# Strassen's weight sums moved to accumulating DMAs, and one product added onto another's PSUM bank

## The chip, the core and the metric

The kernel runs on one core of one Trainium2 chip. The metric is device time in microseconds for one execution, as the median of several runs. TensorE is called PE, VectorE DVE, ScalarE ACT, GpSimd POOL and SyncE SP, as in the profile.

## The reference

One layer of a streaming encoder for 512 tokens and a model dimension of 2048, all in float32. Cut to what matters:

```python
hn   = rmsnorm(x, norm_g)                                   # (512, 2048)
proj = hn @ w_in                                            # 3 branches x (q, k, v, gate) x 4 heads x 128 columns,
                                                            # 4 forget logits, 3 x 2048 merge gate logits
ya = forgetting_attention(qa, ka, va, f_logit)              # branch A
yb = chunked_relpos_attention(qb, kb, vb, rel_bias)         # branch B
yc = stick_breaking_attention(qc, kc, vc)                   # branch C
ys = stack([ya, yb, yc]) * silu(gate path)
merged = sum over branches of sigmoid(merge gates) * (ys @ w_up)
out = x + merged @ w_out
```

Almost all arithmetic is in the projections: `hn @ w_in` (2048 x 12292), `ys @ w_up` and `merged @ w_out`.

## The kernel before

Tokens lie along the free dimension (512 columns), rows of a weight matrix along the partitions. A column tile is 128 output columns; its weights are two loads of 128 x (8 x 128) float32, 512 KB each, one for each half of the 2048 rows. Each factor is split into a high part (float32r, a rounded copy made on ACT, L92) and a low part (the difference, on DVE, L93), and a product is three matmuls, high x high, low x high and high x low (`mm3`, L100 to L103).

**Pairs.** Two column tiles are computed together by Strassen's scheme in Winograd's form (`pair_task`): seven products of half the rows by half the tokens (256 columns) in place of eight. With A11, A12 the first tile's two halves of the rows, and A21, A22 the second's, the products are numbered Q1 to Q7. Their weights are A11 (Q1), A12 (Q2), A22 (Q4) and four sums and differences (Q5, Q7, Q6, Q3). On the other side stand halves of x and differences of them, split once (`combos` for x, `merged_combos` for the merged branches). `combos` makes the differences on POOL, `merged_combos` on DVE. There are 54 pairs: 46 over the columns of `w_in` and 8 over `w_out`. One of them, the first of the output projection, is `late`, with another order of the products, since its operands with x differences are ready last.

**Units.** The work is a list of units; a unit is one stretch of PE with one stationary operand: a product of a pair (24 matmuls of 256 columns), half of a column tile as it stands (the first head's four tiles, 24 matmuls of 512 columns), or half of an up projection (18 matmuls of 512 columns). The loop at the end of `hybrid_kernel` goes over the units: it first emits the splits (`prep_to`) of up to two units ahead, then the loads (`load_to`) of up to six ahead, then the unit's matmuls, its eviction (`after`) and the stages of attention that hang on it (`side`). A scheduler orders the instructions on each engine by their dependences and its own costs; PE keeps the written order only for the first 17 units.

**Buffers.** Raw weights have six buffers (`raw`), split weights three for the high and three for the low part (`wh`, `wl`), projections four PSUM banks (`acc`), and temporaries of 128 x 512 share 21 slots (`t2`). So a split waits until PE has finished the unit three before it.

**A pair before.** All four loads are issued on SP for the first unit. On DVE, w5 = A21 + A22 (L315), w7 = w1 - w7 (L324), w6 = w5 - w1 (L325) and w3 = w3 - w6 (L327), each 128 x 1024; the late pair makes the same sums by L315, L317, L318 and L327. The order of the products is Q1, Q2, Q6, Q7, Q4, Q5, Q3. Evictions are one copy on ACT and seven additions or subtractions of 128 x 256 on DVE.

**The start.** The rows of x come in by 16 loads, are split raw, and the first head's four column tiles run on them as they stand, while the norm is found; then `combos` multiplies x by its norm (DVE, L255), makes the differences (POOL, L257 to L260), and the parts are split again (x1h, x1l, t23h, t23l, x2h, x2l). The first pair needs these.

Of the kernel before, what the change touches and what calls it, by code (L numbers as in the profile page):

```python
# [38 lines left out]
def hybrid_kernel(  # L39
# [60 lines left out]
    def mm3(ps, lh, ll, rh, rl, start, stop):  # L100
        nc.tensor.matmul(ps, lh, rh, start=start, stop=False)  # L101
        nc.tensor.matmul(ps, lh, rl, start=False, stop=False)  # L102
        nc.tensor.matmul(ps, ll, rh, start=False, stop=stop)  # L103

    # ------------------------------------------------------------------ constants
# [18 lines left out]
    class Unit:  # L124
        """A stretch of the tensor engine's work with one stationary operand of up to 8 k tiles."""

        def __init__(self, shape, prep, mms, srcs=(), after=None):
            self.shape, self.prep, self.mms, self.srcs, self.after = shape, prep, mms, srcs, after
            self.hi = self.lo = None
# [4 lines left out]
    def load(u):  # L134
        u.raw = []
        for s, keep in u.srcs:
            t = raw_tile(u.shape)
            nc.sync.dma_start(t, s)
            u.raw.append(t)
            if keep is not None:  # L140
                keep.append(t)
# [8 lines left out]
    def prep_raw(u):  # L150
        split_to(u.hi, u.lo, u.raw[0])
# [21 lines left out]
    # -1 where key k >= j: suffix sums inside a block  # L173
# [4 lines left out]
    # A, rows are queries: NEG where the key (free) is after the query  # L178
# [4 lines left out]
    # C, rows are keys: valid where the query (free) is after the key  # L183
# [7 lines left out]
    # column h has ones on the rows h, 32 + h, 64 + h, 96 + h  # L191
# [6 lines left out]
    # the query gains carry the softmax scale  # L198
# [33 lines left out]
    def rsqrt(y, ps, n):  # L232
        """y = (ps / n + EPS) ** -0.5: a guess by exp and ln, and one Newton step."""
# [17 lines left out]
    def combos(k):  # L251
        """The rows of x at their norm, and what Strassen's form needs of them beside the parts."""
# [5 lines left out]
        nc.gpsimd.tensor_sub(a[:, RH], a[:, RH], a[:, LH])  # L258
        nc.gpsimd.tensor_sub(t[:, LH], b[:, RH], a[:, RH])
# [24 lines left out]
    def col_task(srcs, xs, evac):  # L284
        """A column tile as it stands; two units, one for each half of the rows."""
        ps = Lazy(acc)

        def mms(i):
            def go(u):
                for j in range(UK):  # L290
# [4 lines left out]
                     srcs=[(srcs[i], None)],  # L295
                     after=(lambda: evac(ps())) if i == 1 else None) for i in range(2)]

    def pair_task(src1, src2, ops, done, late=False, before_last=None):
        """Two column tiles by seven products in place of eight (Strassen, in Winograd's form).

        late: the products with T2, T3 and T4 come last."""
        kept = []
        st = {}
        w = {}
        order = (1, 2, 5, 3, 6, 7, 4) if late else (1, 2, 6, 7, 4, 5, 3)

        def prep_of(i):
            p = order[i]

            def go(u):  # L310
                if i == 0:
                    w[1], a21, w[4], w[2] = kept
                    split_to(u.hi, u.lo, w[1])
                    w[5] = raw_tile()
                    nc.vector.tensor_add(w[5], a21, w[4])  # L315
                    if late:
                        nc.vector.tensor_sub(a21, w[1], a21)  # L317
                        nc.vector.tensor_sub(w[1], w[5], w[1])  # L318
                    w[7], w[6], w[3] = a21, w[1], w[2]
                    return  # L320
                split_to(u.hi, u.lo, w[p])
                if i == 1:
                    if not late:
                        nc.vector.tensor_sub(w[7], w[1], w[7])  # L324
                        nc.vector.tensor_sub(w[6], w[5], w[1])  # L325
                if i == (1 if late else 4):
                    nc.vector.tensor_sub(w[3], w[3], w[6])  # L327
            return go

        def mms_of(i):  # L330
            def go(u):
                st["ps"] = ps = acc()[:, LH]
                for j in range(UK):
                    mm3(ps, u.hi[:, j, :], u.lo[:, j, :], *ops[order[i]](j), j == 0, j == UK - 1)
            return go

        def after_of(i):
            p = order[i]

            def go():  # L340
                ps = st["ps"]
# [8 lines left out]
                elif p == 6:  # L350
                    add(u[:, LH], u[:, LH], ps)
                    if late:
                        add(c1[:, RH], c1[:, RH], u[:, LH])
                elif p == 7:
                    add(u[:, RH], u[:, LH], ps)
                    if late:
                        add(c2[:, RH], c2[:, RH], u[:, RH])
# [4 lines left out]
                elif p == 5:  # L362
# [548 lines left out]
```

## Time and profile before

| | |
|---|---|
| median of 3 runs | 1400.05 us (1399.22 to 1400.08) |
| profiled execution | span 1397.6 us from the first to the last instruction; its own whole time is not on the page |
| busy: PE, DVE, ACT, POOL | 1366.3, 1191.8, 729.7, 53.7 us |
| mean granted PE clock | 0.995 |
| moved by DMA | 176.39 MB, 126 GB/s in the mean, 38.4% of the DMA engines' time on SP's and ACT's load queue |

The span is from the first to the last instruction; busy is the time with an instruction under way. Matmuls overlap, so the pace of PE is read from the distance of their starts. A wait is shown as who waited, and for whom (`<-`); a releaser is inferred.

### The profile page before, as it was taken

The numbers are of one execution on the slowest core, as the hardware profiler recorded it, in microseconds if no ns is written. First come the engines' busy times: TensorE is split into PE (matmuls) and PEld (weight loads), VectorE is DVE, ScalarE is ACT, GpSimd is POOL, SyncE is SP. The second block draws the span as 40 slices with busy tenths as digits, with TensorE's granted clock in tenths as the row PEclk, the third lists the DMA queues.
The fourth block names the chain that finished last, engine by engine and source line by source line (L and its number), as shares of the span: only waits on it lengthen the run. The fifth ranks groups of instructions, "written<-read, shape, count | busy, mean of one in ns | idle before, by whom it ended". The sixth has DMA issues, their size and how long they took to land.

```text
span 1397.6 us, 25474 instructions
## 1 busy us (share of the span) xinstructions
PE 1366.3 (98%) x10452; PEld 1316.7 (94%) x10452; DVE 1191.8 (85%) x1671; ACT 729.7 (52%) x1042; POOL 53.7 (4%) x60
## 2 busy tenths in 40 slices
PE   6969999999999999999999999999999999999999
PEld 3759999999999999999999999999999988899999
DVE  8999898887978889888888888888888888898886
ACT  6345564544545555555556555545555755453332
POOL 4730000000000000000000000000000000000000
PEclk9989999999999999999999999999999999999999
DMA  7113334323344244342433333333233766535542
GB/s 272 46 46 106 122 102 126 121 91 114 106 129 126 95 114 128 113 129 95 117 122 115 121 94 119 113 114 121 91 115 103 273 197 203 169 109 176 164 151 76
DMA packets 63093, 176.39 MB, mean 126 GB/s; under 512 B 7400, under 2 KB 9320, under 8 KB 62976
## 3 DMA queue, kind: packets, MB, share of 16 engines
q1 hardware_dynamic: 59520, 170.49, 38.4%
q10 hardware_dynamic: 3456, 4.26, 0.8%
q8 instruction: 82, 1.34, 0.4%
q14 instruction: 35, 0.29, 0.1%
HBM read 155.04 MB, written 19.69 MB: 125 GB/s over the span
## 4 chain that ended last, share of the span: by engine, by line
PE 92%; DVE 5%; issue 1%; ACT 0%; POOL 0%; DMA 0%; SPq 0%; DVEq 0%; ACTq 0%; POOLq 0%
PE acc L101 27%; PE acc L103 27%; PE acc L102 27%; PE att L103 3%; PE att L101 3%; PE att L102 3%; DVE x L255 1%; DVE wl L93 1%; PE att L548 1%; PE att L517 1%; PE att L570 1%; DVE x1l L93 1%; PE att L571 1%; PE att L569 1%; DVE t23l L93 0%
## 5 line engine op out<-in xcount | busy, mean ns | idle before, releaser
L92 ACT ACTIVATE wh<-raw 128x1024 fp32r<-128x1024 f32 (+1 forms) x418 | 435.7, 1043 | 549.2 <-PE acc L102 488.2
L93 DVE TENSOR_TENSOR wl<-raw,wh 128x1024 fp32r<-128x1024 f32 (+1 forms) x418 | 503.9, 1206 | 96.7 <-ACT wh L92 95.9
L102 PE MATMUL acc<-x1l,wh 128*128 128x256 f32 (+1 forms) x768 | 222.3, 289 | 10.5 <-DVE x1l L93 10.5
L103 PE MATMUL acc<-x1h,wl 128*128 128x256 f32 (+1 forms) x768 | 222.0, 289 | 2.2 <-DVE wl L93 2.2
L101 PE MATMUL acc<-x1h,wh 128*128 128x256 f32 (+1 forms) x768 | 223.7, 291 | 0.0
L101 PE MATMUL acc<-x2h,wh 128*128 128x256 f32 (+1 forms) x768 | 223.6, 291 | 0.0
L102 PE MATMUL acc<-x2l,wh 128*128 128x256 f32 (+1 forms) x768 | 221.9, 289 | 0.9 <-DVE x2l L93 0.9
L103 PE MATMUL acc<-x2h,wl 128*128 128x256 f32 (+1 forms) x768 | 221.8, 289 | 0.0
L101 PE MATMUL acc<-t23h,wh 128*128 128x256 f32 x736 | 209.7, 285 | 0.0
L103 PE MATMUL acc<-t23h,wl 128*128 128x256 f32 x736 | 208.4, 284 | 0.0
L102 PE MATMUL acc<-t23l,wh 128*128 128x256 f32 x736 | 208.1, 283 | 0.0
L102 PEld LDWEIGHTS acc<-x1l,wh 128*128 128x128 f32 x768 | 147.8, 192 | 13.4 <-DVE x1l L93 11.2
L103 PEld LDWEIGHTS acc<-x1h,wl 128*128 128x128 f32 x768 | 147.8, 193 | 3.9 <-DVE wl L93 2.4
L102 PEld LDWEIGHTS acc<-x2l,wh 128*128 128x128 f32 x768 | 148.0, 193 | 2.4 <-DVE x2l L93 1.1
L101 PEld LDWEIGHTS acc<-x1h,wh 128*128 128x128 f32 x768 | 147.9, 193 | 1.8 <-issue 0.2
L101 PEld LDWEIGHTS acc<-x2h,wh 128*128 128x128 f32 x768 | 148.2, 193 | 1.3
L103 PEld LDWEIGHTS acc<-x2h,wl 128*128 128x128 f32 x768 | 148.0, 193 | 1.3
L101 PEld LDWEIGHTS acc<-t23h,wh 128*128 128x128 f32 x736 | 141.0, 192 | 0.5
L102 PEld LDWEIGHTS acc<-t23l,wh 128*128 128x128 f32 x736 | 141.0, 192 | 0.1
L103 PEld LDWEIGHTS acc<-t23h,wl 128*128 128x128 f32 x736 | 140.7, 191 | 0.3
L101 PE MATMUL acc<-t,wh 128*128 128x256 f32 x368 | 105.1, 286 | 0.0
L102 PE MATMUL acc<-t,wh 128*128 128x256 f32 x368 | 104.4, 284 | 0.0
(256 smaller groups left out, 2728.0 us busy)
## 6 DMA issues: line engine op xcount, KB each, us to landing
raw<-in_w_col SPq DMA_DIRECT2D x192, 512.0 KB, 3.6
raw<-in_w_out SPq DMA_DIRECT2D x32, 512.0 KB, 3.8
gl<-c SPq DMA_DIRECT2D x48, 256.0 KB, 2.0
raw<-in_w_up SPq DMA_DIRECT2D x32, 384.0 KB, 3.2
sg<-gl SPq DMA_DIRECT2D x48, 256.0 KB, 5.0
x<-in_xT SPq DMA_DIRECT2D x16, 256.0 KB, 5.4
xr<-in_xT SPq DMA_DIRECT2D x16, 256.0 KB, 4.4
yd<-y SPq DMA_DIRECT2D x11, 256.0 KB, 2.0
```

Of the source, the lines that this page charges most:

```text
L92: nc.scalar.activation(hi, src, AF.Copy)
L93: nc.vector.tensor_sub(lo, src, f(hi))
L101: nc.tensor.matmul(ps, lh, rh, start=start, stop=False)
L102: nc.tensor.matmul(ps, lh, rl, start=False, stop=False)
L103: nc.tensor.matmul(ps, ll, rh, start=False, stop=stop)
L255: nc.vector.scalar_tensor_tensor(x, x, gn[:, kt:kt + 1], rstd[0], op0=ALU.mult, op1=ALU.mult)
L517: nc.tensor.transpose(ps[:, blk(i)], st["p"][i][:, blk(j)], identf)
L548: nc.tensor.matmul(ps[:, i * P:], nu_r if i == j else nones_r, part, start=i == j and part is st["lk"][j][0], stop=False)
L569: nc.tensor.matmul(o, vh[:, blk(j)], st["h"][j], start=j == 0, stop=False)
L570: nc.tensor.matmul(o, vl[:, blk(j)], st["h"][j], start=False, stop=False)
L571: nc.tensor.matmul(o, vh[:, blk(j)], st["l"][j], start=False, stop=j == QB - 1)
```

## The change

The signs of the differences of x and of the merged branches are turned, so that every weight sum is a plain addition: w5 = A21 + A22, w7 = A11 + A21, w6 = w5 + A11, w3 = w6 + A12. In a normal pair w5 and w7 are made by the loads: a plain load on SP, then a DMA from POOL that adds the second part onto the buffer. w6 and w3 are made on DVE in the buffer of w5 after its split (L332 and L335 of the changed kernel). In the late pair all four sums are made by DMAs: w3 by one load and three adds, w6 by one and two, w5 and w7 by one and one. The loads are issued unit by unit and no longer all with the first: 5 plain and 2 adding loads in a normal pair, 7 and 7 in the late one.

The order of the products is Q5, Q1, Q2, Q6, Q7, Q4, Q3 in a normal pair and Q1, Q2, Q3, Q5, Q6, Q7, Q4 in the late one. In a normal pair Q5 stays in its PSUM bank; DVE reads the bank once after Q7 (L367), and Q3's matmuls are then added onto the bank (`more`: its first matmul doesn't start a new sum). One addition on DVE falls away. Comments and docstrings are blanked out as well.

```diff
-    def mm3(ps, lh, ll, rh, rl, start, stop):
+    def mm3(ps, lh, ll, rh, rl, start, stop, more=False):
...
-        nc.gpsimd.tensor_sub(a[:, RH], a[:, RH], a[:, LH])
-        nc.gpsimd.tensor_sub(t[:, LH], b[:, RH], a[:, RH])
+        nc.gpsimd.tensor_sub(a[:, RH], a[:, LH], a[:, RH])
+        nc.gpsimd.tensor_add(t[:, LH], b[:, RH], a[:, RH])
...
-        order = (1, 2, 5, 3, 6, 7, 4) if late else (1, 2, 6, 7, 4, 5, 3)
+        order = (1, 2, 3, 5, 6, 7, 4) if late else (5, 1, 2, 6, 7, 4, 3)
+        (a11, a12), (a21, a22) = src1, src2
+        parts = {1: [a11], 2: [a12], 4: [a22], 5: [a21, a22], 7: [a11, a21]}
+        if late:
+            parts.update({6: [a21, a22, a11], 3: [a21, a22, a11, a12]})
+
+        def load_of(i):
+            def go(u):
+                p = order[i]
+                if p not in parts:
+                    return
+                w[p] = raw_tile()
+                nc.sync.dma_start(w[p], parts[p][0])
+                for src in parts[p][1:]:
+                    nc.gpsimd.dma_start(w[p], src, accum_op=ALU.add)        # L322
+            return go
...
             def go(u):
-                if i == 0:
-                    w[1], a21, w[4], w[2] = kept
-                    split_to(u.hi, u.lo, w[1])
-                    w[5] = raw_tile()
-                    nc.vector.tensor_add(w[5], a21, w[4])
-                    if late:
-                        nc.vector.tensor_sub(a21, w[1], a21)
-                        nc.vector.tensor_sub(w[1], w[5], w[1])
-                    w[7], w[6], w[3] = a21, w[1], w[2]
-                    return
                 split_to(u.hi, u.lo, w[p])
-                if i == 1:
-                    if not late:
-                        nc.vector.tensor_sub(w[7], w[1], w[7])
-                        nc.vector.tensor_sub(w[6], w[5], w[1])
-                if i == (1 if late else 4):
-                    nc.vector.tensor_sub(w[3], w[3], w[6])
+                if not late and p == 1:
+                    w[6] = w[5]
+                    nc.vector.tensor_add(w[6], w[6], w[1])                  # L332
+                elif not late and p == 6:
+                    w[3] = w[6]
+                    nc.vector.tensor_add(w[3], w[3], w[2])                  # L335
...
-                st["ps"] = ps = acc()[:, LH]
+                more = p == 3 and not late
+                st[p] = ps = st[5] if more else acc()[:, LH]
...
                 elif p == 6:
-                    add(u[:, LH], u[:, LH], ps)
+                    sub(u[:, LH], ps, u[:, LH])
                     if late:
-                        add(c1[:, RH], c1[:, RH], u[:, LH])
+                        sub(c1[:, RH], c1[:, RH], u[:, LH])
                 elif p == 7:
-                    add(u[:, RH], u[:, LH], ps)
-                    if late:
-                        add(c2[:, RH], c2[:, RH], u[:, RH])
+                    sub(u[:, RH], u[:, LH], ps)                             # L366
+                    sub(c2[:, RH], u[:, RH], c2[:, RH] if late else st[5])  # L367
...
                 elif p == 5 and late:
                     nc.scalar.activation(c2[:, RH], ps, AF.Copy)
-                elif p == 5:
-                    add(c2[:, RH], u[:, RH], ps)
-                    add(u[:, LH], u[:, LH], ps)
-                elif late:
-                    add(c1[:, RH], c2[:, RH], ps)
-                else:
-                    add(c1[:, RH], u[:, LH], ps)
+                    add(c1[:, RH], c1[:, RH], ps)
+                elif p == 3 and late:
+                    nc.scalar.activation(c1[:, RH], ps, AF.Copy)
+                elif p == 3:
+                    sub(c1[:, RH], ps, u[:, LH])
```

`merged_combos` changes as `combos` does, and `rest` of the output projection takes its addend off instead of adding it for that half, with `u` in place of the finished sum.

More of the change, by code (lines that the diff above doesn't have):

```diff
@@ L134, in load @@
     def load(u):
[L135 to L141, printed above, removed]
+        if u.load is not None:
+            u.load(u)
+        elif u.src is not None:
+            u.raw = raw_tile(u.shape)
+            nc.sync.dma_start(u.raw, u.src)
     def prep(u):
@@ L340, in go @@
             def go():
[L341 removed]
+                ps = st[p]
                 if i == 0:
@@ L373, in after_of @@
             return go
-        src = {0: [(src1[0], kept), (src2[0], kept), (src2[1], kept), (src1[1], kept)]}
-        return [Unit([UK, P], prep_of(i), mms_of(i), srcs=src.get(i, ()), after=after_of(i)) for i in range(7)]
+        return [Unit([UK, P], prep_of(i), mms_of(i), load=load_of(i), after=after_of(i)) for i in range(7)]
     side = {}
```

30 lines of the change are left out of this document (15 added, 15 removed).

## The prediction

> **What bounds the kernel now.** I read the page's busy shares first, then busy time by stretch, then the waits of the tensor engine (PE), then the timelines where it waits. The page, busy time in 13 stretches from 100 us on (one stretch, then the sum), and PE's waits before and after 100 us:
>
> ```profile
> span 1397.6 us, 25474 instructions
> PE 1366.3 (98%) x10452; PEld 1316.7 (94%) x10452; DVE 1191.8 (85%) x1671; ACT 729.7 (52%) x1042; POOL 53.7 (4%) x60
> 400.00:500.00 100.00, 100.00 (x823) 99.40 (x822) 83.78 (x119) 54.17 (x76) 0.00 (x0) 1.00 0.39 122
> sum 1297.00, PE 1292.34 PEld 1262.22 DVE 1098.28 ACT 680.09 POOL 1.51; mean PE 99.41 PEld 97.09 DVE 84.48 ACT 52.31 POOL 0.12
> PE acc L102 <- DVE x1l L93: 10.5, 2, 6.3
> PE acc L103 <- DVE wl L93: 2.2, 1, 2.2
> PE acc L102 <- DVE x2l L93: 0.9, 1, 0.9
> PE acc L103 <- DVE wl L93: 1.0, 2, 0.8
> PE acc L101 <- ACT wh L92: 1.0, 2, 0.6
> ```
>
> The columns of a stretch are its length, then PE, PEld, DVE, ACT and POOL busy, the granted clock and DMA. PE is busy in all 100 us of a middle stretch at clock 1.00 and for 1292.34 of the last 1297 us. Here a relieved vector engine (DVE) buys nothing. What can be won is little: 10.5 + 2.2 + 0.9 us of waits for DVE before 100 us (the first three waits), and 1.0 + 1.0 us later (the last two), where the output projection begins.
>
> PE's pace, from four pairs of rows: 256 columns in the middle, 512 columns, and 256 columns at the reduced clock:
>
> ```profile
> 699.79 0.28 PE L101 MATMUL acc<-x2h,wh 128*128 128x256 f32 x1
> 702.31 0.28 PE L101 MATMUL acc<-x1h,wh 128*128 128x256 f32 x1
> 61.19 0.39 PE L101 MATMUL acc<-x2h,wh 128*128 128x512 f32 x1
> 65.72 0.39 PE L103 MATMUL acc<-x2h,wl 128*128 128x512 f32 x1
> 88.75 0.58 PE L102 MATMUL acc<-x1l,wh 128*128 128x256 f32 x1 [6.27 <-DVE x1l L93]
> 92.97 0.41 PE L103 MATMUL acc<-x2h,wl 128*128 128x256 f32 x1
> 93.18 0.41 PE L101 MATMUL acc<-x2h,wh 128*128 128x256 f32 x1
> ```
>
> 21 matmuls in 2.52 us are 0.12 us each, so a product of 24 takes 2.88 us and a pair of seven products 20.2 us; 54 pairs are 1089 us of the span, and the change leaves their matmuls as they are. 20 of 512 columns in 4.53 us are 0.227 each, so an up projection's unit of 18 takes 4.1 us.
>
> **The middle: removed work that was hidden, added work to be hidden.** A normal pair (53 of 54) loses two weight sums and one addition on DVE; the other two sums stay, as L332 and L335 (these, L366 and L367 are lines of the changed kernel, the rest of the one before):
>
> ```profile
> L93 DVE TENSOR_TENSOR wl<-raw,wh 128x1024 fp32r<-128x1024 f32 x386 | 473.4, 1226 | 85.3 <-ACT wh L92 84.5
> L92 ACT ACTIVATE wh<-raw 128x1024 fp32r<-128x1024 f32 x386 | 408.8, 1060 | 521.2 <-PE acc L102 488.2 <-issue 16.8 <-DVE wl L93 5.8
> L315 DVE TENSOR_TENSOR raw<-raw,raw 128x1024 f32<-128x1024 f32 x54 | 66.6, 1233 | 1.8 <-DMA raw<-in_w_out 0.7
> L364 DVE TENSOR_TENSOR u<-u,acc 128x256 f32<-128x256 f32 x53 | 22.0, 414 | 0.0
> raw<-in_w_col SPq DMA_DIRECT2D x192, 512.0 KB, 3.6
> gl<-c SPq DMA_DIRECT2D x48, 256.0 KB, 2.0
> ```
>
> 53 x (2 x 1.23 + 0.41) = 152 us of DVE time go. Worth: 0, since PE never waits there; nor can it cost. The changed signs keep every instruction's shape, and the late pair's one more copy on ACT stands beside PE: 0. Added: 56 more plain loads on SP (53 pairs x 1, late pair 3) and 113 accumulating ones on POOL (53 x 2 + 7), 512 KB each. The cover is the buffer's turn: the built order shows each raw buffer refilled right after its split and wanted again one pair later, 20.2 us; off go the plain load (3.6) and the split (1.06 + 1.23), which leaves 14.3 us for one add. The order also shows each add alone on POOL behind its own load, with the gate stores ahead on SP as before.
>
> No row shows an accumulating DMA. It must read the half already in SBUF besides; below it is a plain load, 3.6 us, above I take three passes, 10.8 us. I take 5.6: the load, and a read from SBUF, whose nearest row is the store gl<-c, 2.0 us. All are under 14.3, so the middle costs nothing by this.
>
> New is that PE waits for DVE: Q3 adds onto Q5's bank, so its first matmul waits until L367 has read the bank, queued on DVE behind whatever stands there; behind Q3 stand the next pair's products. In order, Q4 (2.88 us) covers L366 and L367 (0.8 us). In 11 pairs, one a head, the built order puts L367 behind the next pair's splits (its destination waits for a free slot) and Q3 behind the next Q5 and Q1. Q3 then holds one of three wh/wl buffers, and Q1's split must fit into Q5's 2.88 us: 2.88 - 1.06 - 1.23 leaves 0.6. Bounds: 0, and one more DVE operation of 1.23 in the way, (1.23 - 0.6) x 11 = 7 us. I take 0.8, since DVE's share from 100 us on falls from 84% to some 74% ((1098 - 141) / 1297, where 141 of the 152 lie).
>
> **The start: the gain.** Rows of DVE's timeline, then of POOL's:
>
> ```profile
> 52.83 1.22 DVE L93 TENSOR_TENSOR wl<-raw,wh 128x1024 fp32r<-128x1024 f32 x1
> ...
> 57.89 0.69 DVE L93 TENSOR_TENSOR t23l<-t,t23h 128x512 fp32r<-128x512 f32 x1 [2.12 <-ACT t23h L92]
> 59.38 1.76 DVE L315 TENSOR_TENSOR raw<-raw,raw 128x1024 f32<-128x1024 f32 x1
> 61.06 0.68 DVE L626 TENSOR_TENSOR c<-acc,rstd 128x512 f32<-128x512 f32 x1
> 61.67 1.21 DVE L324 TENSOR_TENSOR raw<-raw,raw 128x1024 f32<-128x1024 f32 x1
> 62.80 1.23 DVE L93 TENSOR_TENSOR t23l<-t,t23h 128x512 fp32r<-128x512 f32 x1
> 63.95 1.21 DVE L93 TENSOR_TENSOR wl<-raw,wh 128x1024 fp32r<-128x1024 f32 x1
> ...
> 77.68 1.74 DVE L325 TENSOR_TENSOR raw<-raw,raw 128x1024 f32<-128x1024 f32 x1
> 84.74 1.21 DVE L327 TENSOR_TENSOR raw<-raw,raw 128x1024 f32<-128x1024 f32 x1
> 88.02 0.68 DVE L93 TENSOR_TENSOR x1l<-x,x1h 128x512 fp32r<-128x512 f32 x1
> 57.27 0.74 POOL L260 TENSOR_TENSOR t<-t,x 128x256 f32<-128x256 f32 x1
> 60.14 1.61 POOL L259 TENSOR_TENSOR t<-x,x 128x256 f32<-128x256 f32 x1
> 64.17 1.59 POOL L257 TENSOR_TENSOR t<-x,x 128x256 f32<-128x256 f32 x1 [0.70 <-DVE t23l L93]
> 70.17 1.06 POOL L258 TENSOR_TENSOR x<-x 128x256 f32<-128x256 f32 x1
> ...
> 80.08 0.78 POOL L258 TENSOR_TENSOR x<-x 128x256 f32<-128x256 f32 x1
> ```
>
> PE's 6.27 us end with the x1l of 88.02, the eighth k tile, and DVE has no gap from 57.89 to there: its queue is the bound. All four sums of the first pair lie in that stretch. In the built order L315, L324 and L327 are gone from it and L332 stands where L325 did. Of L315 and L324 (1.76 + 1.21) not all comes back: the t23l of 62.80 waits for POOL's L259 by way of ACT. With L315 and L324 out of its way POOL should need 0.74 there (L260 alone) and not 1.61 (beside DVE), so t23l starts some 1.2 us earlier. L327 gives another 1.2. So x1l ends 2.4 us earlier, and PE's wait with it. Then Q1, which needs x1 only, follows Q5, where Q2 followed Q1 and waited 0.9 for x2l: that wait goes too. Start: -3.3 us.
>
> POOL gets two accumulating DMAs in the midst of these subtractions. Their plain loads refill buffers split at 52.83 and 63.95, so they land at about 57.7 and 68.8 (split 1.2, load 3.6); POOL is there at some 61 (L259 of 60.14) and 71 (L258 of 70.17), so it loses its issue only. No row prices that; POOL has from 80.86 (end of its last L258) to 85.6 (88.02 less 2.4), 4.7 us, or 2.3 an issue, before it counts. I take 0. What is late next is DVE itself.
>
> ```profile
> 66.50:80.20 13.70, 8.52 (x45) 6.93 (x43) 13.70 (x12) 8.17 (x14) 12.99 (x13) 1.00 0.11 35
> 80.20:93.80 13.60, 6.06 (x26) 5.76 (x27) 13.60 (x20) 6.43 (x11) 3.31 (x3) 0.50 0.01 2
> ```
>
> The granted clock is 0.50 from 80.2 to 93.8, after PE's gaps, and matmuls are 0.21 apart there (92.97 to 93.18); 5 us of work after 88.75 end it. My sum keeps that slow stretch as long as it is, from the restart on. The Trainium skill, TensorE: Matmul & The Clock Gate, Part 1: a free-running window of about 3.4 us that is busy throughout restores the clock. The trace agrees so far as 93.8 - 88.75 holds one such window; by that rule a restart at 86.4 could have the clock back one window earlier, and the sum would be 1.5 us lower.
>
> **The output projection.** Its first pair (late) had four sums at DVE's fullest place, and PE's 1.0 + 1.0 us of waits are for DVE and ACT there. Now none is left on DVE: -2.0 at most, I take -1.5, as other work of DVE stays there. But Q3's weights are now one load and three adds in a row, and Q6's one and two. The built order frees Q3's buffer six up units before its split is due: 6 x 4.1 = 24.6, less 3.6 for the load and 1.2 for the split that frees it: 19.8 us, 6.6 an add. At 5.6 it holds. At the end one subtraction stands for one addition: 0.
>
> **Sum.** -3.3 - 1.5 + 0.8 = -4.0 us on the span of 1397.6. The page gives no time for that execution beside its span; the runs, 1399.22 to 1400.08, lie 1.6 to 2.5 us above it, and I carry that over. 1400.05 - 4.0 = **1396.0 us**.
>
> **Rivals.** What a measurement here can tell from no change is 0.2%, 2.8 us.
> - *The adds are too slow* (slower). Place: Q3's chain of three ahead of the output projection. It decides from 6.6 us an add, and each us more costs 3. At 10.8 us: +12.6, less the start's 3.3 and without the -1.5: 1409.4. Over 14.3 us every pair would stall. For it: no row shows such a DMA, and POOL slows beside DVE (0.74 against 1.61). Against: DMA is at 0.39 of its time in the middle. Chance 0.15. The Trainium skill, SBUF — State Buffer, "SBUF: two separate sides", warns against just this: a DMA issued from POOL starves while DVE holds their shared port in a two-port mode. Its section "Who interferes with whom" says that tensor_tensor has no such mode, and tensor_tensor is nearly all that DVE runs here; no run yet shows such a DMA.
> - *The new order stalls PE* (slower): Q3 behind L367 and the tight split, at its bound of 7 us: 1400.05 - 4.8 + 7 = 1402.3. For: 0.6 us of room only. Against: PE has no gap in the middle now with DVE at 84%. Chance 0.15.
> - *Nothing to see*: POOL's issues (over 2.3 us each) or POOL's share of the chain eat the start's gain: 1400.05 - 1.5 + 0.8 = 1399.4, within 1398 to 1401. Chance 0.18.
> - *The sums aren't gone*: excluded, the built order has 1506 rows on DVE against 1671.
>
> **Chances.** The forecast has 0.52, its own range 1393.0 to 1397.2: at its low end the slow-clock stretch is 2.4 us shorter too (2.4 x (1 - 0.12 / 0.21) = 1.0 more), output -2.0, middle 0, and 0.7 for the estimate of POOL's part. Faster 0.52, same 0.2 (nothing to see, and a little of the new order), slower 0.28 (the adds, most of the new order). The range reaches to the rivals until the slower half of the slow adds is left out: 1393 to 1407.
>
> **What would show it.** Right: PE's longest wait for x1l falls from 6.27 to about 4 us, the x2l wait is gone, PE has no gap from 110 to 1190 us, DVE's share is near 74%, an add lands in 4 to 6.6 us, and PE's waits where the output projection begins are under 1 us. Wrong: PE waits for wl or wh once a head (the new order), or for an add ahead of the late pair's Q3 (slow adds), or POOL's last L257 ends after 85 us.

## The result, and the profile after

The changed kernel takes 1414.37 us (median of 4 runs, 1413.88 to 1415.28) against 1400.07 us: a ratio of 1.0103, interval 1.0089 to 1.0117. It is 14.3 us slower; 4.0 us faster had been forecast, with a range up to 1407. The page:

```profile
span 1412.3 us, 25849 instructions
PE 1372.8 (97%) x10452; PEld 1321.8 (94%) x10452; DVE 1071.0 (76%) x1508; ACT 733.4 (52%) x1045; POOL 149.5 (11%) x173
```

DVE is busy 121 us less, and it bought nothing. The first row here is a stretch of the changed kernel, the second of the kernel before: length, then PE, PEld, DVE, ACT and POOL busy, granted clock, DMA share, GB/s.

```profile
100.00:400.00 300.00, 292.56 (x2377) 290.45 (x2377) 221.23 (x327) 149.08 (x224) 22.41 (x26) 0.99 0.69 177
```
```profile
100.00:400.00 300.00, 300.00 (x2474) 298.78 (x2473) 259.46 (x373) 153.38 (x226) 0.00 (x0) 1.00 0.36 111
```

PE used to be busy in all 300 us. Now 7.4 us are missing, with 97 matmuls fewer. PE's waits from 100 us on in the changed kernel (total, times, longest):

```profile
PE att L555 <- ACT lkh L92: 7.4, 4, 2.0
PE acc L102 <- ACT m2h L92: 3.3, 1, 3.3
PE att L102 <- ACT yh L92: 0.9, 1, 0.9
PE acc L104 <- DVE wl L93: 0.2, 1, 0.2
PE att L103 <- DVE yl L93: 0.2, 1, 0.2
```

But for the 0.2 us for wl, none of these is for a weight. L555 sums the lk tiles in the four heads of branch C (`stick_sums`), and lkh is their high part, made on ACT. (m2h is the high part of an operand that Q2 of the late pair takes; yh and yl are operands of the up projections.)

**Where the time went.** Both kernels have 10452 matmuls on PE. The start of the n-th in one trace less the start of the n-th in the other is how far the one is behind, and steps in that distance give each place its price:

| place | forecast | measured |
|---|---|---|
| until the first head's tiles run | 0 | +0.6 |
| start (first pair) | -3.3 | -2.7 |
| heads of branch C, 100 to 400 us | part of +0.8 | +11.5 |
| heads of branches B and A, 400 to 1095 us | part of +0.8 | 0.0 |
| start of the up projections | 0 | +1.9 |
| start of the output projection | -1.5 | +2.7 |
| end, mostly the last store (2.7 to 3.4 us) | 0 | +0.7 |
| sum | -4.0 | +14.7 |

**Why 7.4 us of waits cost 11.5.** Four windows of the changed kernel's PE clock:

```profile
188.40:191.81 3.41, 2.32 (x20) 2.12 (x18) 2.62 (x6) 1.59 (x3) 0.00 (x0) 1.00 0.82 306
191.81:195.23 3.42, 2.54 (x21) 2.50 (x22) 3.42 (x7) 1.60 (x5) 0.86 (x1) 1.00 0.71 218
280.52:283.93 3.41, 1.45 (x12) 1.20 (x10) 2.63 (x6) 2.26 (x4) 0.42 (x1) 1.00 0.82 267
283.93:287.35 3.42, 3.42 (x19) 3.42 (x18) 1.38 (x5) 0.62 (x2) 0.50 (x2) 0.50 0.95 207
```

The wait is the same 1.96 us both times. At 190.7 it falls across two windows, which keep 2.32 and 2.54 us of work, and nothing follows. At 280.8 it falls into one, which keeps 1.45, and the next window runs at clock 0.50 with 19 matmuls: 1.7 us more. That happens twice. 7.4 and 3.4 are 10.8 us; the other 0.7 is not put down to anything here.

### The profile page after: what moved, and what is told of

The parts are those of the page before. It is cut to its first block, busy times and chain, and to the rows that moved or that the text cites. A ratio compares the mean times of both kernels' runs of the same rounds, so it can differ in the third digit from the quotient of the medians.

```text
span 1412.3 us, 25849 instructions
## 1 busy us (share of the span) xinstructions
PE 1372.8 (97%) x10452; PEld 1321.8 (94%) x10452; DVE 1071.0 (76%) x1508; ACT 733.4 (52%) x1045; POOL 149.5 (11%) x173
## 4 chain that ended last, share of the span: by engine, by line
PE 90%; DVE 4%; DMA 2%; ACT 1%; issue 1%; POOL 1%; SPq 0%; POOLq 0%; DVEq 0%; ACTq 0%
PE acc L102 26%; PE acc L103 26%; PE acc L104 26%; PE att L103 2%; PE att L104 2%; PE att L102 2%; DMA raw<-in_w_out 1%; DVE x L254 1%; PE att L555 1%; DVE wl L93 1%; PE att L524 1%; ACT wh L92 1%; PE att L577 1%; PE att L578 0%; DVE x1l L93 0%
## 5 line engine op out<-in xcount | busy, mean ns | idle before, releaser
L322 POOL DMA_DIRECT2D raw<-in_w_col x92 | 79.6, 865 | 920.8 <-DMA raw<-in_w_col 505.7
L102 PE MATMUL acc<-t,wh 128*128 128x256 f32 x368 | 105.6, 287 | 0.0
```

Source lines behind the costliest of these rows:

```text
L102: nc.tensor.matmul(ps, lh, rh, start=start, stop=False, skip_group_check=more)
L322: nc.gpsimd.dma_start(w[p], src, accum_op=ALU.add)
```

## The experiments

Four columns of the table are steps of the same distance to the kernel before, in us: start, heads of branch C, start of the up projections, start of the output projection. "New order" is Q5 first, as changed; "own bank" means that Q3 is not added onto Q5's bank.

| kernel | time | start | C heads | up | output |
|---|---|---|---|---|---|
| as changed | 1414.4 | -2.7 | +11.5 | +1.9 | +2.7 |
| e1 sums written a unit later | 1414.4 | -2.7 | +11.5 | +1.1 | +2.5 |
| e2 own bank | 1412.6 | -2.8 | +9.4 | +1.2 | +3.6 |
| e3 late pair on DVE | 1408.8 | -2.8 | +11.6 | +1.8 | -1.3 |
| e4 normal pairs' sums on DVE | 1418.7 | -2.2 | +16.7 | 0.0 | +3.3 |
| e5 old order, own bank | 1405.6 | +0.9 | 0.0 | 0.0 | +3.5 |
| e7 e5, late pair on DVE | 1399.3 | -0.6 | 0.0 | 0.0 | -1.3 |
| e8 e3, lkh on DVE | 1416.4 | -2.7 | +19.0 | +1.5 | -1.2 |
| e9 e3, PE as written | 1415.4 | -2.8 | +16.7 | +1.6 | -1.3 |
| e10 e9, gates later | 1414.5 | -2.7 | +18.2 | 0.0 | -1.3 |
| e11 e7, first pair in new order | 1397.0 | -2.8 | 0.0 | 0.0 | -1.3 |
| e12 e10, own bank | 1413.3 | -2.8 | +16.2 | 0.0 | -1.3 |
| e13 e11, no accumulating DMA | 1398.1 | -1.9 | 0.0 | 0.0 | +0.1 |
| e14 e3, five banks | 1397.8 | -2.4 | -0.1 | +1.5 | -1.3 |
| e15 e14, gates later | 1396.3 | -2.7 | -0.1 | 0.0 | -1.2 |
| e16 kernel before, five banks | 1399.5 | 0.0 | -0.2 | -0.1 | 0.0 |
| e17 e3, Q5 copied out at once, own bank | 1402.0 | -2.9 | +5.6 | +0.4 | -1.3 |

### First round: place, bank, late chain, adds

**e1, the sums written a unit later**, against the changed kernel:

```diff
-            g += [(OFF["ct"] + i, stick_sums(i)) for i in range(QB)]
+            g += [(OFF["ct"] + (h > 0) + i, stick_sums(i)) for i in range(QB)]
```


> Edit: in heads 1 to 3 of the third attention type the stage that sums the lk tiles on PE (L555) comes one unit of weights later; nothing else changes. In the changed kernel PE waits there four times (1.55, 1.96, 1.96, 1.96 us), and two of the waits are followed by 3.4 us at half clock: the time lost against the kernel before grows by 1.9, 2.1, 3.8 and 3.7 us at these four places. Theory A (the lk chain on ACT and DVE ends under 2 us too late for the place at which PE takes it): one product of 2.88 us more in front of the sums covers it, three of four waits and both stretches of half clock go, -9.6 us, 1404.8 us. Rival B (ACT and DVE are behind altogether in these stretches, the place doesn't matter): the wait moves to another instruction, 1412 to 1416 us.

Measured 1414.37 us (ratio 1.0105, 1.0088 to 1.0122): the four waits are there unchanged, 1.55 and three times 1.96 us. The scheduler puts the first sums behind Q6 of the next pair here as well, so this edit did not move what it was meant to move and leaves theory A untested.

**e2, own bank**, against the changed kernel:

```diff
-                more = p == 3 and not late
+                more = False
...
+                    if not late:
+                        sub(u[:, LH], st[5], u[:, LH])
...
-                    sub(c1[:, RH], ps, u[:, LH])
+                    add(c1[:, RH], u[:, LH], ps)
```


> Edit: Q3 gets a PSUM bank of its own again, and one DVE subtraction (0.41 us) per normal pair takes Q5's bank into u; signs, order of the products and accumulating DMAs stay. In the built order four weight splits stood on ACT between the last score tile and the last lkh of such a head with the shared bank, two stand there now, as in the kernel before. Theory A1 (the shared bank does it: Q3 is put behind the next pair's Q5 and half of Q1, the splits pile up on ACT ahead of lkh, each waiting for a product to end): all four waits at L555 go with their half clock, -11.4 us, 1403.0 us. Rival A2 (the accumulating DMAs deliver weights too late and hold ACT's queue): the waits stay, 1413 to 1416 us.

Measured 1412.57 us (1.0097, 1.0078 to 1.0117): neither. The built order (the order of each engine's instructions in the built program) was misread there: in the trace the last lkh still stands behind the split that Q6's end releases. The three waits of 1.96 us are 1.55 now, and the first, 1.55, is 2.03. That Q3 shares Q5's bank isn't the cause by itself; Q5 still holds its bank until DVE has read it behind Q7.

**e3, the late pair's sums on DVE**, against the changed kernel:

```diff
+                if late:
+                    if i == 0:
+                        for q, src in ((1, a11), (7, a21), (4, a22), (2, a12)):
+                            w[q] = raw_tile()
+                            nc.sync.dma_start(w[q], src)
+                    return
...
+                if late and p == 1:
+                    w[5] = raw_tile()
+                    nc.vector.tensor_add(w[5], w[7], w[4])
+                    nc.vector.tensor_add(w[7], w[7], w[1])
... (w6 and w3 likewise)
```


> Edit: the late pair alone (first pair of the output projection) loads its four parts once and makes its four sums on DVE; no accumulating DMA there, order of the products and evictions as changed. Theory C (the chain of three accumulating DMAs, 3.3 + 6.6 to 9.3 us each, lands its last add at 1248.1, ACT's split waits 5.5 us for it with m2h queued behind, PE waits 3.3 us and then has 3.4 us at half clock): the place stops costing 2.7 us and gains nothing on the kernel before, 1411.7 us; the wait of ACT for raw goes. Rival D (ACT's queue is late there for the gates sg, not for the adds): 1414 us, PE still waits about 3 us for m2h.

Measured 1408.83 us (1.0064, 1.0049 to 1.0079): theory C, and 1.3 us better than the kernel before at that place. The chain in the changed kernel, first POOL's adds, then ACT:

```profile
1224.98 0.86 POOL L322 DMA_DIRECT2D raw<-in_w_out  x1 [148.32 <-DVE m L747]
1230.87 0.86 POOL L322 DMA_DIRECT2D raw<-in_w_out  x1 [2.71 <-DMA raw<-in_w_out]
1240.74 0.86 POOL L322 DMA_DIRECT2D raw<-in_w_out  x1 [6.06 <-DMA raw<-in_w_out]
```
```profile
1248.18 1.06 ACT L92 ACTIVATE wh<-raw 128x1024 fp32r<-128x1024 f32 x1 [5.50 <-DMA raw<-in_w_out]
1249.14 0.61 ACT L92 ACTIVATE m2h<-m 128x512 fp32r<-128x512 f32 x1
```

Q3's three adds took 5.9, 9.9 and 7.4 us from issue to issue or split, 23.2 in all, where the forecast had 16.8 and room for 19.8. ACT stood 5.5 us before Q3's split, and m2h, which Q2 needed, stood behind it. The same stretch in the changed kernel and in the kernel before (the last three columns are granted clock, DMA share and GB/s):

```profile
1224.00:1249.00 25.00, 22.52 (x119) 19.30 (x117) 15.55 (x24) 7.85 (x10) 6.07 (x7) 1.00 1.00 250
```
```profile
1224.00:1249.00 25.00, 23.87 (x173) 22.45 (x172) 23.37 (x36) 15.91 (x27) 0.00 (x0) 1.00 0.33 109
```

The DMA engines are busy all the time while the chain runs. The first of the three adds landed in 5.6 us, the next two, with others under way, in 9.3 and 7.3.

**e4, the normal pairs' sums on DVE**, against the changed kernel:

```diff
+                if not late:
+                    if i == 0:
+                        for q, src in ((7, a21), (4, a22), (1, a11), (2, a12)):
+                            w[q] = raw_tile()
+                            nc.sync.dma_start(w[q], src)
+                    return
...
+                if not late and p == 5:
+                    w[5] = raw_tile()
+                    nc.vector.tensor_add(w[5], w[7], w[4])
... (w7 += w1 with Q1)
```


> Edit: in the normal pairs the two weight sums come from DVE instead of accumulating DMAs (four plain loads, two more additions of 1.23 us a pair); order, signs, shared bank and the late pair as changed. Theory A1 (shared bank): the built order still has four splits ahead of the last lkh, the four waits at L555 stay; the start's gain of 2.7 us goes, since the first pair's sums are back in DVE's queue: 1417 us. Rival A2 (accumulating DMAs): the waits at L555 go, 1414.4 - 11.4 + 2.7 = 1405.7 us.

Measured 1418.74 us (1.0135, 1.0119 to 1.015): A2 falls, the waits grow (10.3 us, the longest 4.4) without the normal pairs' adds. But the start kept -2.2 of its -2.7 us with the sums back on DVE.

### Second round: the order of the products

**e5, the old order**, against the changed kernel:

```diff
-        order = (1, 2, 3, 5, 6, 7, 4) if late else (5, 1, 2, 6, 7, 4, 3)
+        order = (1, 2, 3, 5, 6, 7, 4) if late else (1, 2, 6, 7, 4, 5, 3)
... (each product its own bank, w5 still loaded with the first unit)
```


> Edit: normal pairs take their products in the order of the kernel before (1,2,6,7,4,5,3), each with its own bank; the signs and all accumulating DMAs stay as changed, the late pair too. The run with the sums one unit later left all four waits at L555 as they were, the one with an own bank left three at 1.55 us: neither the unit nor the shared bank decides. Theory E (the new order of the products: on PE the lk sums stand right behind one product, Q6 of the next pair, whose end releases a split of 1.06 us on ACT that stands ahead of the last lkh, so PE always waits for split and lkh): with the old order the sums stand behind Q7, a product later, and the waits go; start -1.5 to -2.5, late pair's chain of adds still +3 to +4: 1400 to 1402.5 us. Rival F (the accumulating DMAs hold ACT and DVE up): the waits stay, 1408 to 1412 us.

Measured 1405.60 us (1.004, 1.0026 to 1.0054). PE's waits from 100 us on, and the adds' issues (count, KB, median us to landing):

```profile
PE acc L102 <- ACT m2h L92: 4.2, 1, 4.2
PE acc L104 <- DVE wl L93: 0.8, 1, 0.8
```
```profile
raw<-in_w_col POOLq DMA_DIRECT2D x92, 512.0 KB, 5.9
```

From 110 us to the output projection the distance to the kernel before stands still, with 90 adds in that stretch (all 92 of the normal pairs over `w_in` but the first pair's two): they cost nothing there. F falls; the order of the products makes the waits. The total lies above what theory E gave: the start gained nothing, and the one wait for wl, in the output projection, came with 1.4 us more.

**e7, the old order and the late pair on DVE**: e5's edit and e3's.

> Edit: as the kernel with the old order of the products and own banks, and the late pair's four sums on DVE from four plain loads. Theories E and C together (order costs the middle, the chain of adds costs the output projection's start, the adds of the normal pairs cost nothing): start -1.5 to -2.5, middle 0, output projection -1.3: 1396 to 1398 us. Rival F: 1405 us or more.

Measured 1399.27 us (0.9996, 0.9987 to 1.0006): theories E and C at their places; the start again fell short, by 0.9 us or more, and the output projection gives back 0.6 us of its 1.3 further on.

**e8, lkh on DVE**, against e3:

```diff
-                split_to(*st["lk"][j], t)
+                hi, lo = st["lk"][j]
+                nc.vector.tensor_copy(hi, t)
+                nc.vector.tensor_sub(lo, t, f(hi))
```


> Edit: order of products, shared bank and adds of the normal pairs as changed, late pair on DVE as in the run before (1408.8 us); the high part of the four lk tiles of such a head is written by DVE instead of ACT. Theory E (lkh stands on ACT behind a split that waits for PE's product): PE's place for the sums is the same in the built order, lkh no longer waits for that split; each wait falls from 1.96 to 0.5 to 1.2 us and no stretch at half clock follows, 1403 to 1406 us. Rival G (DVE's part of the lk chain is what is late): waits of 1.9 us and more, 1408 to 1411 us.

Measured 1416.43 us (1.0118, 1.0103 to 1.0133): theory E's number is wrong, the waits are 2.63 us. DVE just after Q6's end at 379.2:

```profile
379.43 0.35 DVE L562 CAST lkh<-lk 128x384 fp32r<-128x384 f32 x1
380.30 1.23 DVE L93 TENSOR_TENSOR wl<-raw,wh 128x1024 fp32r<-128x1024 f32 x1 [0.52 <-ACT wh L92]
381.44 0.42 DVE L562 CAST lkh<-lk 128x512 fp32r<-128x512 f32 x1
```

The second lkh moved from behind that split's wh to behind its wl. The wait is what stands in the queue: here 1.06 (wh) + 1.23 (wl) + 0.42 less the overlaps, in the changed kernel 1.06 + 1.03, in e2 1.06 + 0.61.

### Third round: PE's order, the table loads, the first pair

**e9, PE as written**, against e3:

```diff
-OFF = dict(..., man=17, ...)
+OFF = dict(..., man=110, ...)
```


> Edit: PE's instructions keep the order in which the program writes them through unit 110 (all heads of the third attention type) instead of unit 17; Q5 first, the shared bank and the normal pairs' adds stay as changed, the late pair's sums on DVE (base 1408.8 us). In the built order the lk sums then stand behind Q7 of the next pair and the last lkh behind a split that Q2's end releases, two products earlier; with the planner's order they stood behind Q6 and behind a split that Q6's end releases. Writing lkh on DVE did not help, it stood there behind the same product's wl (wait 2.63 us). Theory E (the pair 'sums behind product n, lkh behind the split that n releases'): all four waits and the half clock go, -11.4 us, 1397.4 us. Rival F2 (Q5 first as such makes the chain late: fewer free slots, Q3 held back for the bank): the waits stay or turn into waits for wh, 1405 to 1412 us.

Measured 1415.37 us (1.0109, 1.0095 to 1.0123): theory E is wrong again. No wait at the sums, but in their stead

```profile
PE acc L102 <- DVE c L383: 7.2, 3, 2.4
PE acc L102 <- DVE c L376: 3.2, 1, 3.2
```

Three times Q3 waits 2.4 us until L383 (L367 of the changed kernel) has read Q5's bank; once Q4 waits 3.2 us for the bank that L376 (L360 of the changed kernel) empties of Q2. The first is the hazard that the prediction named; in the changed kernel the scheduler had avoided it by putting Q3 behind the next Q5 and half of Q1.

**e10, the gates later**, against e9:

```diff
-            at(len(units) - 3, lambda d=d: load_gates(d))
+            at(len(units) - (2 if d == 0 else 3), lambda d=d: load_gates(d))
```


> Edit: as the run with PE's order as written, and the gates of the first up projection are loaded one unit later. In the changed kernel ACT loads its table three times near 1108 us (sigmoid, exponential, sigmoid, 1.28 us each) where the kernel before loads it once, since a sigmoid stands ahead of the last head's exponential; PE then waits 0.9 + 0.2 us and the place costs 1.9 us. In this built order the exponential comes first and one load is left. Theory T (the two table loads are the 1.9 us): 1.5 to 2 us less than the run beside it, 1395.6 us if that is at 1397.4. Rival (the last head's rows yr come late from memory, 5 us a load): no difference.

Measured 1414.54 us (1.0101, 1.0086 to 1.0117). The place itself goes from +1.6 to 0.0, theory T. The whole shows less, since the heads of branch C lose 1.5 us more than in e9: four waits are followed by half clock here, three there. In the changed kernel ACT had

```profile
1108.15 1.28 ACT L742 ACT_TABLE_LOAD   x1
1109.45 0.72 ACT L742 ACTIVATE sg<-sg,small_in 128x512 f32<-128x512 f32 x1
1110.19 1.28 ACT L585 ACT_TABLE_LOAD   x1
1111.48 0.63 ACT L585 ACTIVATE y<-y 128x512 f32<-128x512 f32 x1
1112.13 1.28 ACT L742 ACT_TABLE_LOAD   x1
```

one sigmoid ahead of the last head's exponential, and so two loads of 1.28 us too many in front of yh.

**e11, the first pair alone in the new order**, against e7:

```diff
-        order = (1, 2, 3, 5, 6, 7, 4) if late else (1, 2, 6, 7, 4, 5, 3)
+        order = (1, 2, 3, 5, 6, 7, 4) if late else (5, 1, 2, 6, 7, 4, 3) if first else (1, 2, 6, 7, 4, 5, 3)
...
-                more = False
+                more = p == 3 and first
```


> Edit: the kernel with the old order of products, own banks and the late pair on DVE (1399.3 us), with the first pair alone in the new order (Q5 first, shared bank). The start gained 2.7 us with the new order and accumulating DMAs, 2.2 us with the new order and the sums on DVE, 0.6 us with the old order and accumulating DMAs. Theory S (Q5 and Q1 first, which need x1 alone, make the start's gain, not the sums off DVE): -1.6 to -2.1 us, 1397.4 us. Rival (the gain hangs on all that follows): 1399 us.

Measured 1396.97 us (0.998, 0.9972 to 0.9989): theory S, faster than the kernel before.

### Fourth round: a bank too few

**e12, PE as written and own bank**: e10's edits and e2's.

> Edit: Q5 first in all normal pairs with their accumulating DMAs, own banks, PE's order as written through unit 110, gates of the first up projection one unit later, late pair on DVE. On ACT the built order is that of the run with own banks (the last lkh stands behind the split that Q6's end releases, where PE waited 1.55 us three times); on PE the lk sums now stand behind Q7, one product of 2.88 us later, and no product waits for the reading of another's bank. Theory E (what costs is that the sums stand directly behind the product whose end releases the split ahead of lkh): no wait at L555, middle 0, start -2 to -2.7, output projection -1.3: 1395.5 to 1397.5 us. Rival F2 (Q5 first makes ACT and DVE late in these heads wherever the sums stand): waits of over 1 us again, 1402 to 1412 us.

Measured 1413.32 us (1.0096, 1.0081 to 1.0112): theory E as stated is finished. But the new wait says what is short. PE's longest wait in sum, PE, and ACT:

```profile
PE acc L102 <- ACT u L374: 5.5, 3, 1.8
```
```profile
380.59 0.38 PE L102 MATMUL acc<-t23h,wh 128*128 128x256 f32 x1 [1.82 <-ACT u L374]
```
```profile
378.69 1.06 ACT L92 ACTIVATE wh<-raw 128x1024 fp32r<-128x1024 f32 x1 [1.41 <-PE acc L103]
379.65 0.61 ACT L92 ACTIVATE lkh<-lk 128x512 fp32r<-128x512 f32 x1
380.17 0.36 ACT L374 ACTIVATE u<-acc 128x256 f32<-128x256 f32 x1
```

Q7 (on t23) waits for the copy that empties Q1's PSUM bank, a product that ended two products earlier. Of four banks Q5 holds one, Q1, Q2 and Q6 the others. The copy stands on ACT behind lkh, and lkh behind the split that Q6's end releases.

**e13, no accumulating DMA**, against e11 (the old loop over the parts stands behind the `return` and is never reached):

```diff
-                if late:
-                    if i == 0:
-                        for q, src in ((1, a11), (7, a21), (4, a22), (2, a12)):
-                            w[q] = raw_tile()
-                            nc.sync.dma_start(w[q], src)
-                    return
+                if i == 0:
+                    for q, src in ((1, a11), (7, a21), (4, a22), (2, a12)):
+                        w[q] = raw_tile()
+                        nc.sync.dma_start(w[q], src)
+                return
... (w5 and w7 by tensor_add)
```


> Edit: the fastest run so far (first pair with Q5 first, old order behind it, late pair on DVE, 1397.0 us) with no accumulating DMA at all: each part is loaded once and all four sums of every pair are DVE's, as in the kernel before; the new signs stay. Theory S (the start's gain is the order of the first pair; the sums taken off DVE buy nothing, and 56 loads and 113 adds cost nothing in the middle): 1396.5 to 1398 us. Rival (the first pair's sums in DVE's queue cost the start): -0.5 us of gain only, 1399 to 1400 us.

Measured 1398.09 us (0.9986, 0.9977 to 0.9995): theory S. Against e11 the start gives 0.9 us less and the beginning of the output projection 1.4, of which e11 gives 0.9 back further on.

**e14, five banks for the products**, against e3:

```diff
-    pa = ctx.enter_context(tc.tile_pool(name="pa", bufs=4, space=PS))
-    pt = ctx.enter_context(tc.tile_pool(name="pt", bufs=4, space=PS))
+    pa = ctx.enter_context(tc.tile_pool(name="pa", bufs=5, space=PS))
+    pt = ctx.enter_context(tc.tile_pool(name="pt", bufs=3, space=PS))
```


> Edit: one PSUM bank moves from the attention's pool to the products' (5 and 3 instead of 4 and 4); everything else as in the run with the late pair on DVE (1408.8 us): Q5 first, shared bank, adds, PE's order by the planner. The run with own banks and PE's order as written turned its waits into 1.82 us of Q7 for the ACT copy that empties Q1's bank, queued behind the split that Q6's end releases. Theory K (Q5 first holds Q5's bank from the pair's first product until Q7 or Q3, three of four banks are left, so Q7's bank hangs on ACT's queue, and the planner puts the lk sums in its place, where lkh hangs on the same queue): with a fifth bank the built order has Q6 and Q7 and then the sums, as before the change; the four waits go with their half clock, -11.4 us, 1397.4 us. Rival F2 (the lk chain itself is late with Q5 first): waits of over 1 us stay or move, 1403 us or more.

Measured 1397.77 us (0.999, 0.9981 to 0.9999): theory K, to 0.4 us. First PE's sums and ACT of e14, then the same place in the changed kernel:

```profile
367.70 0.68 PE L571 MATMUL att<-lkh,nu_r 128*128 128x512 f32 x3
```
```profile
365.14 1.06 ACT L92 ACTIVATE wh<-raw 128x1024 fp32r<-128x1024 f32 x1 [2.06 <-PE acc L103]
366.10 1.03 ACT L92 ACTIVATE lkh<-lk 128x384 fp32r<-128x384 f32 x2
367.04 0.36 ACT L374 ACTIVATE u<-acc 128x256 f32<-128x256 f32 x1
```
```profile
374.38 0.50 PE L555 MATMUL att<-lkh,nu_r 128*128 128x512 f32 x1 [1.96 <-ACT lkh L92]
```
```profile
372.34 1.06 ACT L92 ACTIVATE wh<-raw 128x1024 fp32r<-128x1024 f32 x1 [1.82 <-PE acc L103]
373.30 1.03 ACT L92 ACTIVATE lkh<-lk 128x384 fp32r<-128x384 f32 x2
374.23 0.36 ACT L358 ACTIVATE u<-acc 128x256 f32<-128x256 f32 x1
```

ACT's queue is the same: split, two lkh, Q1's copy. But with a fifth bank PE runs Q7 first, and when it comes to the sums, 2.56 us after the split began, lkh is there. Q7 starts at about 365, 2 us before Q1's bank is emptied (the copy of 367.04), so it has the fifth. With four, Q7 has no bank when Q6 ends (Q1's copy is at 374.23), the sums stand in its place, and PE is at them when the split begins.

**e15, five banks and the gates later**: e14's edit, and the gates one unit later as in e10.

> Edit: as the run with five banks for the products, and the gates of the first up projection loaded one unit later, which in the built order leaves one ACT table load of three. Theories K and T: 1.6 us less than the run beside it, 1395.8 us. Rival: no difference.

Measured 1396.27 us (0.9977, 0.9968 to 0.9986), 1.5 us less than e14: theory T, and the fastest kernel here, though its interval overlaps e11's.

**e16, the kernel before with five banks**: e14's edit on the kernel before.

> Edit: the kernel before with five banks for the products and three for the attention, nothing else. A control: theory K has no held bank here, so the fifth bank buys nothing, 1399 to 1401 us. Were it 1396 us or less, the fifth bank would be a gain of its own and not the cure of the change; fewer banks for the attention may also cost, 1402 us.

Measured 1399.54 us (0.9998, 0.9989 to 1.0006): the fifth bank is no gain of its own.

**e17, Q5 copied out at once, own bank**, against e3:

```diff
+                if p == 5 and not late:
+                    nc.scalar.activation(c2[:, RH], ps, AF.Copy)
...
-                    sub(c2[:, RH], u[:, RH], c2[:, RH] if late else st[5])
+                    if not late:
+                        sub(u[:, LH], c2[:, RH], u[:, LH])
+                    sub(c2[:, RH], u[:, RH], c2[:, RH])
```


> Edit: four banks each as changed, but ACT copies Q5's product to c2 at once (0.37 us a pair, u is combined by one more DVE subtraction), Q3 has its own bank; late pair on DVE. The bank is no longer held until Q7, but its release hangs on ACT's queue. In the built order the sums stand behind Q6 again and the last lkh behind Q6's split. Theory K with that order: waits of 1.5 us at L555 stay, 1404 to 1409 us. Rival (freeing the bank early in itself is enough): 1397 to 1399 us.

Measured 1402.02 us (1.0015, 1.0006 to 1.0025). Three waits of 1.55 us at the sums stay, as theory K had it with that order; the time is 2 us under its range, since none of them was followed by half clock and the first head had none. Q5's bank is not free for Q7 there either, since its copy stands on ACT behind the same split and lkh, 1.4 us after Q6's last matmul ends (368.5):

```profile
369.95 0.36 ACT L374 ACTIVATE c<-acc 128x256 f32<-128x256 f32 x1
```

## Why the prediction was wrong, step by step

- **The middle, +0.8: the step that failed.** Q3's bound counted DVE's queue and the three `wh`/`wl` buffers, and left out the four PSUM banks, though holding Q5's is what the change does. The loss is not in 11 pairs and not for a weight: it is in four heads, for lkh or for a bank, 11.5 us with the half clock; e14 ends it, e12 has the wait for the bank itself where Q7 goes first, and e16 shows that a fifth bank buys nothing where Q5's isn't held. The rival *the new order stalls PE* had the right part of the change, the wrong wait, and 7 us as its bound. That the clock falls after a wait of under 2 us was not in any price.
- **The output projection, -1.5: a mis-sized term.** 5.6 us an add were taken, 16.8 for three; they took 23.2. The rival *slow adds* had the place and the rule: 23.2 less 19.8 us of room is 3.4 late, PE waited 3.3, and with the half clock behind it the place lost 4.0 (from -1.3 in e3 to +2.7). That 3.4 and 3.3 agree so closely is partly luck: PE waited not for Q3's weights but for m2h, behind them in ACT's queue. What the rival had against it was the DMA's 0.39 in the middle; where the chain ran the share was 1.00. (Its price, 1409.4, also leaves out the middle's +0.8.) The -1.5 was right with the sums kept on DVE (e3: -1.3).
- **The start, -3.3, measured -2.7: near in size by luck.** The sum had 2.4 us from the sums taken off DVE and 0.9 from the order. With the old order and the sums off DVE the start is +0.9 and -0.6 (e5, e7), and PE's longest wait for x1l is 6.27 us as before; with the new order and the sums on DVE it is -2.2 and -1.9 (e4, e13); with both -2.7. So the order, by which Q5 and Q1 need x1 alone, makes 70 to 80%, and DVE's relief of 2.4 us did not come through by itself: that DVE's queue is the bound there was read too simply. In the changed kernel the longest wait for x1l is 5.5 us and not about 4, and PE goes on at 87.7 against 88.8. POOL's last `x<-x` starts at 80.17 against 80.08, so POOL's subtractions ended no earlier. The wait for x2l is gone, as forecast. The start's slow stretch is as long as before, 13.65 us of half clock in two pieces (3.41 and 10.24), so the 1.5 us that the restart might have won did not come.
- **The adds in the middle, 0: right.** They land in 6.9 us in the median (e5: 5.9) and 9.2 at most, more than the 5.6 taken but under the 14.3 of cover. The loss is without them too (e4), and e5 has them without the loss. POOL's issue took 0.86 us, 0.85 to 1.14, while DVE was 75% busy, nine tenths of it with tensor_tensor: the starving of POOL's DMAs that the Trainium skill, SBUF — State Buffer, "SBUF: two separate sides", warns of is not seen; its "Who interferes with whom" holds here.
- **DVE near 74%: right** (979.48 of 1312 us from 100 us on, 75%), worth 0 in the middle as said. DVE's busy time falls by 121 us and not by 152, since it counts overlapping instructions once; summed over the instructions, DVE's time falls by 154 (1291.8 to 1138.1).
- **Not foreseen:** the table loads, +1.9 (e10, e15). All eight kernels here with three loads at that place lose 0.4 to 1.9 us there, all ten with one lose none. The Trainium skill, ScalarE activation tables: per-element evaluation and per-set limits, "What a function is on this engine", puts functions of two sets one load of 1283 ns apart; the rows above have 1.28 us each.

What e9, e10 and e12 lose in the heads of branch C is, by their traces, waits and half clock: 11.0, 11.0 and 9.7 us of waits, and 3, 4 and 4 windows of 3.41 us at half clock that cost up to 1.7 us each. That is all but 0.4 to 0.6 us of the +16.7, +18.2 and +16.2.

What stays open: why the scheduler lets the lk chain end as late as it does with Q5 first. e14 takes its fifth bank from the attention's pool; e16 shows that this costs nothing in the kernel before, but no run shows whether the smaller pool also moved the sums behind Q7. That e11, e14 and e15 differ by a real amount isn't shown.

## What to carry to other kernels

Holding an accumulator across products takes a bank from the rotation: count the banks as you count buffers, and see which queue the next one to come free hangs on. An instruction behind a split that waits for product n is late for whatever PE does right after product n, on whichever engine it stands (e8). Work moved off an engine that isn't the bound bought nothing here that the runs can tell (e7: 0.9987 to 1.0006), and the order of instructions that comes with the move can cost more than the move is worth. The gain at the start is the order's: e13 has the new order in the first pair without the move and keeps some 70% of e11's gain.

## What the runs showed of the hardware

- A short wait can halve the clock. In windows of 3.41 us at full clock, from 62 us on in all 18 traces, PE idle for 1.69 us or more (half the window, 55 windows) was always followed by half clock in the next, and idle for 1.67 us or less was not, with one exception (1.46 us, e5 at 92.2). A wait of 1.7 to 2 us costs itself, or itself and 1.7 us more, by where it falls. The Trainium skill, TensorE: Matmul & The Clock Gate, Part 1, has the window but speaks of a whole idle window; the traces say half of one.
- An accumulating DMA of 512 KB landed 5.8 to 8.1 us after its issue, in the median of a run's group (8.9 for the seven of e4), and up to 10.2 in the changed kernel; plain loads of that size beside them took 4.0 to 5.2, against 3.6 to 3.9 without adds. Stores got slower beside them, too: the 128 KB output store from 1.7 to 4.4 us in the median.
